# Scoring both heads of an attention pair with 64-row products, the causal mask added to the gate row, and the weight sums of the MLP moved behind the attention

## The chip, the cores and the metric

The kernel runs on one core of one Trainium2 chip. The metric is device time in microseconds (us); before the change the median of three runs is 1742.12 us, with 1740.56 and 1743.21 us at the ends. A core has TensorE (PE: products, and PEld: the loads of their stationary operand), VectorE (DVE), ScalarE (ACT), GpSimd (POOL) and SyncE (SP), whose queue issues every DMA of this kernel.

## The reference

One layer of a hybrid decoder for one sequence of 1024 tokens of width 1024, in float32. A conditioning vector gives shifts, scales and gates. One input projection feeds 16 state-space heads (a chunked scan, "SSD") and 16 attention heads of width 64. The attention is what the change touches; for each block of 128 queries it is

```
logits = einsum('bqhd,bkhd->bhqk', q[:, q0:q1], k[:, :q1]) * d ** -0.5
logits = logits + (cum[:, :, q0:q1, None] - cum[:, :, None, :q1])   # cum: summed log forget gates
logits = where(arange(q0, q1)[:, None] >= arange(q1)[None, :], logits, -inf)
out    = einsum('bhqk,bkhd->bqhd', softmax(logits), v[:, :q1])
```

A term that is the same for all keys of a query drops out of the softmax, so only the key's part of `cum` is needed. The two head groups are normed, joined, and projected by `w_out`; then come a LayerNorm, an MLP of width 4096 with squared ReLU, and a second LayerNorm.

## The kernel before, in words

Each number is kept as a high part (fp32r) and a low part, the remainder, and a product of two numbers is three products of parts: high by high, high by low, low by high. A projection of one 128-column tile over 512 tokens is 8 x 3 products, all 128x128 by 512 columns (`proj`). A planner orders the instructions of each engine from a simulated timeline, by the order in which the program names them and by when operands and buffers come free; the engines then run their lists in that order, and so does SP with its DMAs. `tc.issue_after(x)` (`after` here) keeps DMAs behind `x` in SP's list.

The stages are: conditioning and projections with the SSD scan (to about 385 us), the attention (to about 916 us), the output projection with its norm (to about 1124 us), and the MLP with the second norm. The MLP's products use sums of blocks of its weights (a seven-product scheme): `w2_sums` loads 1 MB of `w2`, makes four differences of 128x512 on POOL, and stores 1 MB to a DRAM scratch `w2t`. There are 14 such calls, two per head pair in the first seven pairs of the attention. They use the buffers `ex` (two).

In the attention, the heads go in 8 pairs. `qkv(p)` projects q, k and v of a pair; it is a generator, advanced in pieces of half a projection (`PIECES`), so that TensorE has these products between those of the attention proper (for the last pair, `out_ssm`, the first half of the output projection). q and k come out with head 0 on partitions 0 to 63 and head 1 on 64 to 127. For each head a tile `q_st` or `k_st` is made that holds the high part in the head's own 64 partitions and the low part in the other 64 (ACT copies the product to `qk_e`, POOL writes the high part, DVE the low part: two 64x512 instructions each per half). One 128-row product of `q_st` with `k_st` is then high by high plus low by low; for the cross terms `swap` makes a copy of the 256 queries with the halves exchanged, by two DMAs of 64 KB, and a second 128-row product uses that copy.

A unit is a head and a group `g` of two query blocks (`tb` = 2g and 2g+1). Pairs run `g` from 0 to 3. `probs` does, for a block of W = 128 (tb + 1) keys, two products per 512 keys, and on the last 128 keys one bf16 product with the identity that adds the mask. Then DVE adds the gate row `cum` and takes the maximum in one pass over W columns (line 519, from PSUM tag `S`, two buffers of 1024 columns: one per head and block), negates the maximum (line 521), ACT takes the exponential and its sum, DVE the reciprocal, and POOL multiplies (line 524). `weigh` transposes the 128x128 blocks on TensorE (line 546), splits them (ACT 548, DVE 549) and multiplies them with v into `o_ps`. The unit after is started before a unit is weighed. `cum` is one row of the DRAM scratch `rowd`, loaded to all partitions, one per head, two buffers.

Of the kernel before, what the change touches and what calls it, by code (L numbers as in the profile page):

```python
# [8 lines left out]
F32 = mybir.dt.float32  # L9
# [3 lines left out]
ALU = mybir.AluOpType  # L13
# [14 lines left out]
NEG = -1.0e30  # L28
# [4 lines left out]
def layer_kernel(ctx, tc, x, xT, cols, rows3, w_ada, b_ada, w_in, w_dtf, w_out, ln_rows, w1, w2, out):  # L33
# [27 lines left out]
    def mm(o, l, r, start, stop):  # L61
        nc.tensor.matmul(o, l, r, start=start, stop=stop)  # L62
# [30 lines left out]
    identb = cst.tile([P, P], BF16, name="identb")  # L93
    nc.vector.tensor_copy(identb, identf)
# [7 lines left out]
    nc.gpsimd.affine_select(maskf, maskf, pattern=[[-1, P]], compare_op=ALU.is_ge, fill=NEG, base=0,  # L102
                            channel_multiplier=1)
    maskb = cst.tile([P, P], BF16, name="maskb")
    nc.vector.tensor_copy(maskb, maskf)
# [67 lines left out]
    def w2_sums():  # L173
# [134 lines left out]
    def row_form(first):  # L308

        rows = T4("misc", "rows")  # L310
        for hb in range(2):
# [3 lines left out]
            nc.vector.tensor_copy(rows[:16, hb * 512:hb * 512 + 512], rp[:16])  # L315
        load(rowd[first:first + 16, :], rows[:16])

    row_form(0)

    def forget_rows():  # L320
# [6 lines left out]
        row_form(16)  # L327
# [112 lines left out]
    for p in range(NPAIR - 1):  # L440
        wn = w_prep(w_in[XI + p + 1])[0]
# [10 lines left out]
    def qkv(p, st):  # L452
# [3 lines left out]
        for n, idx, scale in (("q", KI + p, 0.125), ("k", VI + p, 1.0), ("v", None, None)):  # L456
            w, _ = ws[-1]
            if idx is not None:
                ws.append(w_prep(w_in[idx]))
                marks["w"] = ws[-1][1]  # L460
                st[n] = ts = [R4("qk", f"{n}_st") for _ in range(2)]
# [3 lines left out]
            for half in range(2):  # L465
# [5 lines left out]
                if idx is not None:  # L471
                    e = sm.tile([P, 512], F32, name="qk_e", tag="o_half", bufs=2)
                    nc.scalar.activation(e, o, AF.Copy, scale=scale)
                    for h in range(2):
                        mine = slice(h * 64, h * 64 + 64)
                        other = slice(64 - h * 64, 128 - h * 64)
                        t = ts[h]
# [16 lines left out]
    def probs(st, h, g, cum):  # L494

        q1, k = st["q"][h], st["k"][h]
        q2 = st["q2"].pop((h, g))
        out = []
        for i in range(2):
            tb = 2 * g + i  # L500
            W = (tb + 1) * P
            if g >= 2:
                sp = PT("S", "s_ps", (P, 1024))
                pt = T4("P", "probs")[:, :W]
            elif i == 0:
                sp2 = PT("S", "s_ps", (P, 1024))
                pt2 = T4("P", "probs")
                sp, pt = sp2, pt2[:, :W]
            else:
                sp, pt = sp2[:, 512:], pt2[:, W - P:2 * W - P]  # L510
            for s0 in range(0, W, 512):
                s1 = min(W, s0 + 512)
                last = s1 == W
# [5 lines left out]
            nc.vector.tensor_tensor_reduce(out=pt, in0=sp[:, :W], in1=cum[:, :W], op0=ALU.add,  # L519
                                           op1=ALU.max, scale=1.0, scalar=-3.0e38, accum_out=m[:, 0:1])  # L520
# [726 lines left out]
```

## Time and profile before

| | us |
|---|---|
| median of three runs | 1742.12 |
| the profiled execution | 1744.44 |
| its span, first to last instruction | 1742.7 |
| PE busy | 1654.0 (95%) |
| DVE busy | 1229.9 (71%) |
| POOL busy | 821.6 (47%) |
| ACT busy | 747.2 (43%) |

The profile is of one execution. A product is in flight far longer than it holds the array, so that PE counts as busy while products overlap; how fast products follow each other is read from their start times. A mean in ns is the time of one instruction, not the distance to the next. Idle time is given with what ended it.

### The profile page before, as it was taken

How to read it: one execution, taken by the hardware profiler on the slowest of the kernel's cores; microseconds unless marked ns; L12 is line 12 of the kernel's file. 1: busy time of each engine (PE TensorE's matmuls, PEld its weight loads, DVE VectorE, ACT ScalarE, POOL GpSimd, SP SyncE). 2: the span in 40 equal slices, each digit the busy share in tenths (PEclk: the TensorE clock that was granted, in tenths of full speed). 3: DMA queues.
4: the chain of work that ended last, by engine and by line, in shares of the span. 5: the costliest groups of instructions: out<-in, count | busy, mean ns of one | idle time of the engine just before them, and what ended most of it. 6: DMA issues, size and time to landing. Idle time of an engine off the chain costs nothing.

```text
span 1742.7 us, 22932 instructions
## 1 busy us (share of the span) xinstructions
PE 1654.0 (95%) x8316; PEld 1368.7 (79%) x8316; DVE 1229.9 (71%) x1898; ACT 747.2 (43%) x1321; POOL 821.6 (47%) x670
## 2 busy tenths in 40 slices
PE   8989899899999999999899999799999999999996
PEld 6777787788877878888778887688888878888885
DVE  7755777686777777676665379986767855646668
ACT  3458355414444444444565334633332334343322
POOL 5121332256566466454442345566656624704535
PEclk9999999999999999999999999899999999999998
DMA  8134343334444534434324644043444596676512
GB/s 331 37 123 147 109 145 109 121 130 151 161 142 170 169 134 167 137 121 132 119 97 130 221 157 169 37 175 133 146 143 160 172 340 212 247 242 205 194 36 96
DMA packets 112032, 268.72 MB, mean 154 GB/s; under 512 B 10128, under 2 KB 37008, under 8 KB 111920
## 3 DMA queue, kind: packets, MB, share of 16 engines
q1 hardware_dynamic: 111920, 267.27, 44.2%
q8 instruction: 65, 1.06, 0.3%
q14 instruction: 47, 0.39, 0.1%
HBM read 194.22 MB, written 64.62 MB: 149 GB/s over the span
## 4 chain that ended last, share of the span: by engine, by line
PE 60%; DVE 15%; DMA 8%; ACT 7%; POOL 5%; issue 4%; SPq 0%; DVEq 0%; ACTq 0%; POOLq 0%
PE mm_ps L62 18%; PE f_ps L957 15%; PE s_ps L1073 9%; PE y_ps L1073 7%; PE s_ps L62 5%; PE o_ps L62 4%; DVE ada_red L134 3%; PE t_ps L546 3%; DMA w_b<-in_w_dram 2%; ACT scores L417 2%; POOL w_b L182 2%; DMA raw_ada<-in_w_ada_dram 1%; DVE w_hl L85 1%; DVE conv_a L346 1%; DVE h_hl L85 1%
## 5 line engine op out<-in xcount | busy, mean ns | idle before, releaser
L62 PE MATMUL mm_ps<-h_hl,w_hl 128*128 128x512 f32 x2016 | 504.5, 400 | 10.9 <-POOL w_hl L79 6.1
L62 PEld LDWEIGHTS mm_ps<-h_hl,w_hl 128*128 128x128 f32 x2016 | 373.5, 191 | 88.3 <-POOL w_hl L79 6.9
L85 DVE TENSOR_TENSOR w_op<-raw_w,w_op 128x512 fp32r<-128x512 f32 (+1 forms) x149 | 186.9, 1260 | 23.2 <-ACT w_op L81 22.6
L957 PE MATMUL f_ps<-h_s,w_op 128*128 128x512 f32 x768 | 183.8, 394 | 6.4 <-ACT h_s L81 3.3
L957 PEld LDWEIGHTS f_ps<-h_s,w_op 128*128 128x128 f32 x768 | 146.0, 190 | 38.4 <-ACT h_s L81 3.7
L524 POOL TENSOR_SCALAR probs<-probs,m 128x128 f32<-128x128 f32 (+7 forms) x128 | 104.5, 822 | 127.3 <-DVE m L523 122.8
L81 ACT CAST w_op<-raw_w 128x512 fp32r<-128x512 f32 (+1 forms) x149 | 114.5, 774 | 100.2 <-PE f_ps L957 53.0
L1073 PE MATMUL s_ps<-w_op,a_op 128*128 128x512 f32 x672 | 153.7, 390 | 1.5 <-DVE a_op L85 1.1
L1073 PEld LDWEIGHTS s_ps<-w_op,a_op 128*128 128x128 f32 x672 | 125.9, 188 | 28.8 <-DVE a_op L85 1.6
L79 POOL TENSOR_SCALAR w_hl<-raw_w 128x512 fp32r<-128x512 f32 x86 | 60.5, 705 | 180.0 <-PE mm_ps L62 126.1
L85 DVE TENSOR_TENSOR a_op<-a_ld,a_op 128x1024 fp32r<-128x1024 f32 x53 | 75.5, 1427 | 98.4 <-ACT a_op L81 98.4
L132 POOL TENSOR_TENSOR raw_ada<-raw_ada,c_act 128x1024 f32<-128x1024 f32 x44 | 88.8, 2027 | 117.1 <-DMA raw_ada<-in_w_ada_dram 99.8
L522 ACT ACTIVATE probs<-probs,m 128x128 f32<-128x128 f32 (+7 forms) x128 | 99.1, 775 | 96.8 <-DVE m L521 86.5
L957 PE MATMUL f_ps<-h_hl,w_op 128*128 128x512 f32 x576 | 136.9, 389 | 0.0
L85 DVE TENSOR_TENSOR w_hl<-raw_w,w_hl 128x512 fp32r<-128x512 f32 x88 | 81.5, 929 | 68.5 <-POOL w_hl L79 68.2
L548 ACT CAST pt_hl<-t_ps 128x512 fp32r<-128x512 f32 (+1 forms) x160 | 84.8, 542 | 100.7 <-PE t_ps L546 97.3
L957 PEld LDWEIGHTS f_ps<-h_hl,w_op 128*128 128x128 f32 x576 | 108.0, 188 | 22.4
L81 ACT CAST a_op<-a_ld 128x1024 fp32r<-128x1024 f32 x53 | 55.7, 1054 | 159.7 <-PE s_ps L1073 80.7
L62 PE MATMUL o_ps<-pt_hl,v_s 128*128 128x256 f32 (+1 forms) x640 | 110.9, 300 | 8.7 <-DVE pt_hl L549 5.4
L549 DVE TENSOR_TENSOR pt_hl<-t_ps,pt_hl 128x512 fp32r<-128x512 f32 (+1 forms) x160 | 99.6, 630 | 23.1 <-ACT pt_hl L548 21.6
L519 DVE CUSTOM_DVE_ANT_0 probs<-s_ps,cumrow 128x128 f32<-128x128 f32 (+7 forms) x128 | 94.8, 750 | 28.9 <-PE s_ps L62 20.1
L1073 PE MATMUL y_ps<-w_op,a_op 128*128 128x512 f32 x504 | 114.7, 389 | 0.0
(254 smaller groups left out, 3136.1 us busy)
## 6 DMA issues: line engine op xcount, KB each, us to landing
raw_w<-in_w_dram SPq DMA_DIRECT2D x57, 512.0 KB, 4.3
a_ld<-ad SPq DMA_DIRECT2D x49, 512.0 KB, 4.4
raw_ada<-in_w_ada_dram SPq DMA_DIRECT2D x48, 512.0 KB, 3.6
raw_w<-in_w_in_dram SPq DMA_DIRECT2D x44, 512.0 KB, 3.7
w_b<-in_w_dram SPq DMA_DIRECT2D x14, 1024.0 KB, 8.0
w2t<-w_b SPq DMA_DIRECT2D x14, 1024.0 KB, 4.3
ad<-a_s SPq DMA_DIRECT2D x28, 512.0 KB, 3.4
raw_w<-w2t SPq DMA_DIRECT2D x28, 512.0 KB, 4.8
```

The lines of the kernel that those rows point to most:

```text
L62: nc.tensor.matmul(o, l, r, start=start, stop=stop)
L79: nc.gpsimd.tensor_scalar(hi, raw, 1.0, 1.0, op0=ALU.mult, op1=ALU.mult)
L81: nc.scalar.copy(hi, raw)
L85: eng.tensor_tensor(lo, raw, hi.bitcast(F32), op=ALU.subtract)
L132: nc.gpsimd.tensor_tensor(raw, raw, c_act.unsqueeze(2).broadcast_to([P, KT, P]), op=ALU.mult)
L519: nc.vector.tensor_tensor_reduce(out=pt, in0=sp[:, :W], in1=cum[:, :W], op0=ALU.add, op1=ALU.max, scale=1.0, scalar=-3.0e38, accum_out=m[: ...
L522: nc.scalar.activation(pt, pt, AF.Exp, bias=m[:, 1:2], scale=1.0, accum_out=m[:, 2:3])
L524: nc.gpsimd.tensor_scalar(pt, pt, m[:, 3:4], 1.0, op0=ALU.mult, op1=ALU.mult)
L548: nc.scalar.copy(hl[:, 0, :n], tp[:, :n])
L549: nc.vector.tensor_tensor(hl[:, 1, :n], tp[:, :n], hl[:, 0, :n].bitcast(F32), op=ALU.subtract)
L957: nc.tensor.matmul(o, l, r, start=first and k == 0 and m == 0, stop=last and k == 3 and m == 2, skip_group_check=True)
L1073: nc.tensor.matmul(banks[j], ahl[a_][:, n, js], whl[w_][:, n, :], start=first and d == 0 and n == 0 and m == 0, stop=last and d == ND - 1 ...
```

## The change

- `qkv`: q and k of both heads are split together, 128 partitions at a time, by ACT (high part) and DVE (low part, straight from PSUM). q is scaled by -0.125 in place of 0.125. POOL has no part in it. `swap` and its DMAs are gone.
- `probs` takes one block of both heads. Each head's logits are three products of 64 rows (high by high, high by low, low by high); the two heads alternate, head 0 on rows 0 to 63 of the array, head 1 on rows 64 to 127, into a PSUM buffer each. They are named with raised priority, and the first product of a block is made to wait for the DVE pass of the block before it, for its second head.
- All logits are negated: the row form of the forget sums is written with a minus, DVE takes the minimum, ACT the exponential with scale -1. The step that negated the maximum is gone.
- The mask is no product any more: POOL adds `maskf` (1e30 above the diagonal) to the 128 columns of the block's diagonal in `cum`, 128x128 per head and block. For this the groups run from `g` = 3 down to 0, and the later block of a group first. The columns beyond are not read again.
- The softmax tiles come in turn from the two buffers of `ex` (both heads in one) and from `P`.
- `w2_sums` is called behind the attention: two calls after each remaining block of `out_ssm` and two after each of the first three blocks of the second half of the output projection, one with POOL and one with DVE, loads ordered behind the last store of the attention.
- `PIECES` and the points where a pair's projections must be done are set anew for the new order.

```diff
-    def w2_sums():
+    def w2_sums(eng):
...
-        with after(marks["w"]):
+        with after(marks["last"]):
...
-            nc.gpsimd.tensor_tensor(o, x_, y_, op=ALU.subtract)
+            eng.tensor_tensor(o, x_, y_, op=ALU.subtract)
...
-        for n, idx, scale in (("q", KI + p, 0.125), ("k", VI + p, 1.0), ("v", None, None)):
+        for n, idx, scale in (("q", KI + p, -0.125), ("k", VI + p, None), ("v", None, None)):
...
-                    e = sm.tile([P, 512], F32, name="qk_e", tag="o_half", bufs=2)
-                    nc.scalar.activation(e, o, AF.Copy, scale=scale)
-                    for h in range(2):
...
-                        nc.gpsimd.tensor_scalar(t[mine, hs], e[mine, :], 1.0, 1.0, op0=ALU.mult, op1=ALU.mult)
-                        nc.vector.tensor_tensor(t[other, hs], e[mine, :], t[mine, hs].bitcast(F32), op=ALU.subtract)
+                    split(o, st[n][0][:, hs], st[n][1][:, hs], "act", scale=scale)
...
+    def prob_tiles():
+        steps[0] += 1
+        if steps[0] % 2:
+            t = T4("ex", "probs", shape=(P, 2, 1024))
+            return [t[:, 0, :], t[:, 1, :]]
+        return [T4("P", "probs") for _ in range(2)]
...
-                mm(sp[:, s0:s1], q1[:, tb * P:(tb + 1) * P], k[:, s0:s1], True, False)
-                mm(sp[:, s0:s1], q2[:, i * P:(i + 1) * P], k[:, s0:s1], False, not last)
-                if last:
-                    mm(sp[:, tb * P:W], identb, maskb, False, True)
+                for m, (a, b) in enumerate(((qh, kh), (qh, kl), (ql, kh))):
+                    for h in range(2):
+                        hp = slice(h * 64, h * 64 + 64)
+                        ins = mm(u["sp"][h][:, at + s0:at + s1], a[hp, tb * P:(tb + 1) * P], b[hp, s0:s1], m == 0, m == 2)
+                        if s0 == 0 and m == 0 and h == 0 and "ttr" in marks:
+                            tc.add_manual_dep(ins.ins, marks["ttr"].ins.name, ...
...
+            nc.gpsimd.tensor_tensor(cum[:, tb * P:W], cum[:, tb * P:W], maskf, op=ALU.add)
...
-            nc.vector.tensor_scalar(m[:, 1:2], m[:, 0:1], -1.0, None, op0=ALU.mult)
-            nc.scalar.activation(pt, pt, AF.Exp, bias=m[:, 1:2], scale=1.0, accum_out=m[:, 2:3])
+            nc.scalar.activation(pt, pt, AF.Exp, bias=m[:, 0:1], scale=-1.0, accum_out=m[:, 1:2])
...
-    PIECES = {p: (0, 3, 1, 3) for p in range(NPAIR)}
+    PIECES = {p: {3: (1, 1), 2: (2, 2), 1: (2, 2), 0: (2, 2)} for p in range(NPAIR)}
...
-    units = [(p, g, h) for p in range(NPAIR) for g in range(4) for h in range(2)]
+    units = [dict(p=p, g=g, st=sts[p], pts=[[None, None], [None, None]]) for p in range(NPAIR) for g in (3, 2, 1, 0)]
...
+    for i in (1, 0):
+        start(units[0], i)
+    for n, u in enumerate(units):
...
+        for h in range(2):
+            if nxt is not None:
+                if nxt["p"] != p:
+                    fill_to(nxt["p"], K_DONE)
+                start(nxt, 1 - h)
+            for _ in range(PIECES[p][g][h]):
+                next(fill, None)
+            if g == 3 and p:
+                fill_to(p, 99)
+            weigh(u["st"], h, g, u["pts"][h], ops[:, h, :])
```

## Rows read from the trace of the kernel before

**Rows 1.** The page: busy us of each engine, share of the span, instructions.
```profile
PE 1654.0 (95%) x8316; PEld 1368.7 (79%) x8316; DVE 1229.9 (71%) x1898; ACT 747.2 (43%) x1321; POOL 821.6 (47%) x670
```
**Rows 2.** Busy time of the engines in four stretches; columns in the first line.
```profile
core 0: us, PE busy (x) PEld busy (x) DVE busy (x) ACT busy (x) POOL busy (x), PEclk, DMA share, GB/s
0.00:40.00 40.00, 31.39 (x123) 25.35 (x124) 28.29 (x38) 14.44 (x14) 23.23 (x19) 0.91 0.87 336
385.00:916.00 531.00, 509.03 (x2912) 427.02 (x2911) 384.43 (x889) 255.62 (x548) 287.55 (x307) 0.98 0.42 142
916.00:1080.00 164.00, 160.88 (x769) 133.21 (x768) 103.75 (x137) 72.74 (x134) 68.30 (x53) 1.00 0.53 174
1200.00:1240.00 40.00, 40.00 (x178) 33.10 (x177) 29.19 (x30) 12.59 (x22) 25.55 (x17) 1.00 0.41 145
```
**Rows 3.** The chain of work that ended last, 385 to 916 us, by line.
```profile
by line: PE mm_ps L62 33.8%; PE o_ps L62 11.8%; PE s_ps L62 10.2%; PE t_ps L546 8.1%; DMA w_b<-in_w_dram 5.6%; POOL w_b L182 4.8%; issue 3.1%; DVE probs L519 2.7%; DVE ada_red L134 2.6%; DVE pt_hl L549 2.2%; POOL probs L524 1.8%; DVE w_hl L
```
**Rows 4.** A wait of TensorE, 385 to 916 us: us, times, longest.
```profile
PE s_ps L62 <- DVE m L519: 3.7, 8, 0.7
```
**Rows 5.** TensorE's groups, 385 to 916 us: busy us, mean ns, idle before.
```profile
L62 PE MATMUL mm_ps<-h_hl,w_hl 128*128 128x512 f32 x1062 | 269.6, 399 | 0.0
L62 PE MATMUL o_ps<-pt_hl,v_s 128*128 128x256 f32 x601 | 103.9, 300 | 8.3 <-DVE pt_hl L549 5.1 <-DVE y_attT L566 2.5 <-ACT pt_hl L548 0.4
L546 PE MATMUL t_ps<-identf,probs 128*128 128x128 f32 x546 | 87.3, 279 | 3.3 <-DVE pt_hl L549 2.6 <-DVE v_s L490 0.3 <-POOL probs L524 0.2
L62 PE MATMUL s_ps<-k_st,q_st 128*128 128x512 f32 (+3 forms) x192 | 70.7, 373 | 3.9 <-DVE m L519 3.7
...
L62 PE MATMUL mm_ps<-wo_hl,y_hl 128*128 128x512 f32 x88 | 24.3, 408 | 2.7 <-POOL wo_hl L85 1.0 <-ACT wo_hl L81 0.6 <-DVE wo_hl L88 0.5
```
**Rows 6.** TensorE in order of time around two runs of 64-column products: start, us.
```profile
122.32 1.32 PE L62 MATMUL mm_ps<-h_hl,w_hl 128*128 128x512 f32 x5
123.56 0.43 PE L62 MATMUL s_ps<-scores,xc 128*64 128x128 f32 x2
123.93 2.83 PE L62 MATMUL mm_ps<-h_hl,w_hl 128*128 128x512 f32 x11
...
152.95 1.50 PE L62 MATMUL s_ps<-xd,b_nat 128*128 128x128 f32 x12
154.38 1.97 PE L62 MATMUL s_ps<-scores,xc 128*64 128x128 f32 x32
156.28 0.73 PE L62 MATMUL mm_ps<-h_hl,w_hl 128*128 128x512 f32 x2
```
**Rows 7.** TensorE in order of time: a score product; after its mask, the next.
```profile
604.25 0.40 PE L62 MATMUL s_ps<-k_st,q 128*128 128x512 f32 x1
...
604.61 0.30 PE L546 MATMUL t_ps<-identf,probs 128*128 128x128 f32 x1
```
**Rows 8.** VectorE's groups by shape, 385 to 916 us.
```profile
L549 DVE TENSOR_TENSOR pt_hl<-t_ps,pt_hl 128x512 fp32r<-128x512 f32 x90 | 61.1, 684 | 13.6 <-ACT pt_hl L548 12.8
...
L479 DVE TENSOR_TENSOR q_st<-qk_e,q_st 64x512 fp32r<-64x512 f32 x28 | 26.1, 931 | 1.8 <-POOL q_st L478 1.0
...
L519 DVE CUSTOM_DVE_ANT_0 probs<-s_ps,cumrow 128x1024 f32<-128x1024 f32 x15 | 18.2, 1216 | 3.9 <-PE t_ps L546 3.8
L521 DVE TENSOR_SCALAR m<-m 128x1 f32<-128x1 f32 x127 | 17.8, 146 | 0.9
```
**Rows 9.** GpSimd's groups by shape, 385 to 916 us.
```profile
L182 POOL TENSOR_TENSOR w_b<-w_b 128x512 f32<-128x512 f32 x52 | 71.1, 1375 | 13.8 <-DMA w_b<-in_w_dram 10.7 <-DVE m L523 2.2
...
L478 POOL TENSOR_SCALAR q_st<-qk_e 64x512 fp32r<-64x512 f32 x28 | 20.1, 719 | 7.1 <-ACT qk_e L473 6.0
...
L524 POOL TENSOR_SCALAR probs<-probs,m 128x128 f32<-128x128 f32 x16 | 6.4, 401 | 16.6 <-DVE m L523 16.3 <-PE s_ps L62 0.2
```
**Rows 10.** DMA issues of the page: count, KB each, us to landing.
```profile
w_b<-in_w_dram SPq DMA_DIRECT2D x14, 1024.0 KB, 8.0
...
q<-q_st SPq DMA_DIRECT2D x128, 64.0 KB, 2.6
```

More of the change, by code (lines that the diff above doesn't have):

```diff
@@ L27 @@
 RMS_EPS = 1e-5
-NEG = -1.0e30
+BIG = 1.0e30
 TAPS = None
@@ L61, in mm @@
     def mm(o, l, r, start, stop):
-        nc.tensor.matmul(o, l, r, start=start, stop=stop)
+        return nc.tensor.matmul(o, l, r, start=start, stop=stop)
     def load(o, i):
@@ L306, in layer_kernel, with row_form @@
     rowd = dr.tile([32, T], F32, name="rowd")
-    def row_form(first):
+    def row_form(first, sign):
         rows = T4("misc", "rows")
@@ L460, in qkv @@
                 marks["w"] = ws[-1][1]
-                st[n] = ts = [R4("qk", f"{n}_st") for _ in range(2)]
+                st[n] = [R4("qk", f"{n}_hl") for _ in range(2)]
             else:
@@ L492, in qkv @@
             yield
[L494 to L510, printed above, removed]
+    steps = [0]
@@ new lines, in prob_tiles, with probs @@
+    def prob_tiles():
[4 more added lines that the diff above has]
+        return [T4("P", "probs") for _ in range(2)]
+    def probs(u, i):
+        st, g = u["st"], u["g"]
+        tb = 2 * g + i
+        W = (tb + 1) * P
+        if g >= 2 or "sp" not in u:
+            u["sp"] = [PT("S", "s_ps", (P, 1024)) for _ in range(2)]
+            u["pt"] = prob_tiles()
+        at = 0 if g >= 2 else i * 512
+        (qh, ql), (kh, kl) = st["q"], st["k"]
+        with tc.high_priority(offset=500):
@@ L521, in probs @@
[L521 to L535 removed]
+                for m, (a, b) in enumerate(((qh, kh), (qh, kl), (ql, kh))):
[3 more added lines that the diff above has]
+                        if s0 == 0 and m == 0 and h == 0 and "ttr" in marks:
+                            tc.add_manual_dep(ins.ins, marks["ttr"].ins.name,
+                                              mybir.DependencyInfo(mybir.DependencyClass.Sync, mybir.DependencyReason.DATA),
+                                              reason="both heads' banks are free")
@@ L688, in layer_kernel, with start @@
             ada_some(1)
-    units = [(p, g, h) for p in range(NPAIR) for g in range(4) for h in range(2)]
+    units = [dict(p=p, g=g, st=sts[p], pts=[[None, None], [None, None]]) for p in range(NPAIR) for g in (3, 2, 1, 0)]
     cums = {}
     ys = {}
-    def start(unit):
-        p, g, h = unit
-        if g == 0 and h == 0:
+    def start(u, i):
+        p = u["p"]
+        if p not in cums:
+            cums[p] = []
             for hh in range(2):
@@ L719, in fill_to @@
             next(fill)
-    swap(sts[0], 0, 0)
-    swap(sts[0], 1, 0)
-    pts = start(units[0])
-    ops = None
-    for n, (p, g, h) in enumerate(units):
-        if g == 3 and h == 1 and p + 1 < NPAIR:
-            fill_to(p + 1, QK_DONE if p + 1 < NPAIR - 1 else 99)
-        if n + 2 < len(units):
-            p2, g2, h2_ = units[n + 2]
-            if g2 == 0 and h2_ == 0:
-                fill_to(p2, Q_DONE)
-            swap(sts[p2], h2_, g2)
-        nxt = start(units[n + 1]) if n + 1 < len(units) else None
-        for _ in range(PIECES[p][g]):
-            next(fill, None)
-        if g == 0 and h == 0 and p:
-            fill_to(p, 99)
-        if h == 0:
-            ops = PT("o", "o_ps", (P, 2, 256))
-        weigh(sts[p], h, g, pts, ops[:, h, :])
-        if h == 1:
-            finish(p, g, ops, ys[p])
-            if g in (1, 3) or p == 7:
-                ada_some(2)
-            if g in (0, 2) and p < 7:
-                w2_sums()
-        pts = nxt
+    for i in (1, 0):
+        start(units[0], i)
+    for n, u in enumerate(units):
+        p, g = u["p"], u["g"]
+        nxt = units[n + 1] if n + 1 < len(units) else None
+        ops = PT("o", "o_ps", (P, 2, 256))
+        for h in range(2):
+            if nxt is not None:
[7 more added lines that the diff above has]
+            weigh(u["st"], h, g, u["pts"][h], ops[:, h, :])
+        finish(p, g, ops, ys[p])
+        if g in (0, 2) or p == 7:
+            ada_some(2)
     g2t = cst.tile([P, 8], F32, name="g2t")
@@ L864, in layer_kernel @@
             u = u_pre(tb + 1)
+        if tb < 3:
+            w2_sums(nc.gpsimd)
+            w2_sums(nc.vector)
     adr = [dr.tile([7, P, 2, 512], F32, name=f"ad{i}") for i in range(ND)]
```

53 lines of the change are left out of this document (18 added, 35 removed).

## The prediction, as it went on record before the changed kernel was run

> **What bounds the kernel now.** I read the page first: PE is busy for 95% of the span (its weight loads, which run beside its products, for 79%), the next engine, DVE, for 71% [rows 1]. Then a table by stage, because a share over the whole span mixes stages. In the attention (385 to 916 us) PE is busy 509 of 531 us, DVE 384, POOL 288; in the output projection behind it PE 161 of 164 us, DVE 104, POOL 68 [rows 2]. TensorE sets both. But "busy" is not "at its pace". The pace stands in a stretch where nothing disturbs PE: 178 products of 512 columns in 40.0 us, 0.225 us each, at a granted clock of 1.00 [rows 2]. Narrow full-array products go no faster than 0.11 us: twelve from 152.95 us, the next group at 154.38, which is 0.119 each with the change of group in it [rows 6]. So I take 0.225, 0.169, 0.1125 and 0.11 us for 512, 384, 256 and 128 columns.
>
> At this pace the attention's list would take: 1150 wide products (1062 + 88) x 0.225 = 259 us; 601 of `o_ps` x 0.1125 = 68; 546 transposes x 0.11 = 60 [rows 5]; the scores with their masks 86 (below); the other hundred or so of the 2912, 11. Sum 484 of 531 us. The remaining 47 us are idle (22), restarts after waits, and some time at half clock (granted 0.98 in the mean, so below 2.4 GHz for a few stretches). That is all that relief of the other engines can give.
>
> Where does the relief lie? The chain that ended last, in this stretch, runs over the weight sums: 5.6% on their loads and 4.8% on their POOL instructions, 55 us of 531 [rows 3]. POOL works in order: a softmax multiply behind a `w_b` difference that still waits for its DMA waits too, and the transposes after it. PE covers most of that with projections.
>
> **The change part by part.**
>
> *The score products.* A pair has 12 chunks of keys per pass over its 8 blocks: six of 512 columns, two each of 384, 256 and 128. One product over each is 6 x 0.225 + 2 x (0.169 + 0.1125 + 0.11) = 2.13 us. Before, two heads with two products each: 4 x 2.13 x 8 pairs = 68 us. A mask costs what it delays the next start: 0.36 us from a 512-column product over its mask to the next, less 0.225, is 0.135 us [rows 7]; 128 of them are 17 us (8 us if one costs only the 0.06 of a half-array product, rows 6). Before: 86 us (76 to 86).
>
> After, six products per chunk for two heads, each with half of the rows. The trace has none of 64 rows, but it has 64-column ones of alternating halves: 32 of 128 columns from 154.38 to 156.28 us, 0.059 us each against 0.119 for the full-array ones before them [rows 6]. Two halves take the time of one whole: they run side by side. If row halves do the same, a pair of them costs what one product cost: 3 x 2.13 x 8 = 51 us. Lower bound: this. Upper: no overlap, 102 us. Between: only the loads of stationary operands go one after the other, no pair under 2 x 0.11 us: 36 pairs per head pair at 0.225 x 8 = 65 us. I take 51, the nearest row.
>
> Going into half-array products and out again is not free. Five wide products from 122.32 us should have let the next start at 123.45; it started at 123.56. Two halves (0.12) should have ended at 123.68; the next wide one started at 123.93 [rows 6]. That is 0.36 us for one excursion. The wide one after the long run shows one more part: its successor starts 0.33 us behind it (0.73 less the 0.40 of one, rows 5 and 6), 0.1 over the pace. So 0.25 to 0.47 us; I take 0.36. There is one run per block, 64 of them, if the planner keeps them whole: 23 us (16 to 30). After: 74 us. The step gives -11 us (ends: 51 + 16 - 86 = -19 and 65 + 30 - 76 = +19; without overlap 102 + 23 - 86 = +39).
>
> *A rule against it.* In rows 2 a wide product hides its weight load entirely, same rows of the array or not (PEld 33.1 us busy beside 178 products in 40.0). The Trainium skill ("TensorE: Matmul & The Clock Gate", Part 3, The mechanism) says that a weight load overlaps products in flight only when their row groups differ. By that rule, with both row halves in flight, each pair would also pay a load. It is a rival below.
>
> *q and k split for both heads.* DVE: 64 instructions of 64x512 at 0.93 become 32 of 128x512; nearest row the one that also reads PSUM, 0.684 [rows 8]: -60 + 22 = -38 us. POOL: 64 x 0.72 = -46 us [rows 9]. ACT unchanged. The projection's only bank is now held until DVE has read it, 0.7 us longer, 32 times; the next half projection is behind other products in PE's list, which cover it. Uncovered it would be 22 us.
>
> *Negated logits.* 128 negations go: -18 us of DVE [rows 8].
>
> *Mask on POOL.* 128 additions of 128x128, not in the trace: between a multiply of that size, 0.40, and a four times larger two-operand one, 1.375 [rows 9]; I take 0.6, near the former: +77 us (51 to 176). The DVE pass must wait for it. It can run from the end of the previous pass of its head, beside the block's own products (0.33 us for the smallest run, 1.35 for the largest), so mostly hidden; where POOL is on a 1.4 us instruction, not.
>
> *Swaps.* 128 DMAs of 64 KB leave SP's list [rows 10]; PE hardly waited for them. Nothing.
>
> *The wait for both passes.* A run's first product waits for both DVE passes of the block before, where each head had its own buffer. Behind it in PE's list everything waits. DVE passes take up to 1.2 us [rows 8]; before, PE waited for them 8 times, 3.7 us in all [rows 4]. The planner puts the run where it expects the pass to be over: I take +4 us (0 to 48, rival below).
>
> *Sums moved.* The attention loses 71 us of POOL [rows 9] and 28 DMAs of 1 MB [rows 10]. With the other edits POOL goes from 288 to about 248 us, DVE from 384 to 328. How much of the 47 us does that give back? At least none, at most some 35 (products will still restart after waits). Since a tenth of the chain lay on the sums, a quarter: -10.
>
> Behind the attention, 14 calls: by the generator's count ten fall into blocks 3 to 7 of the first half, four into the second half. 28 differences each for DVE (at 0.684, +19 on 104) and POOL (at 1.375, +39 on 68) fit into 164 us. DMA is tighter: 174 GB/s x 164 us is 28.5 MB, plus 29.4 MB makes 58; at the rate of the first stretch (336 GB/s at a share of 0.87, so 386 at most) that is 150 of 164 us [rows 2]. The `y_raw` and weight loads that feed PE share SP's list and the engines with it. +5 us (0 to +25).
>
> **Sum**: -11 - 10 + 4 + 5 = -12 us from the profiled execution's 1744.4 (span 1742.7 and 1.7 around it), 1732. That execution lies 2.3 us over the median of 1742.1, so 1730.
>
> **The rivals.**
> 1. *Deeper relief.* Nearly all that is not pace comes back: -35 in place of -10, nothing lost behind: 1742 - 11 - 35 + 4 = 1700. For it: the chain over `w_b`. Against: only 22 us of the stage are idle on PE.
> 2. *A wash.* The restarts eat the score gain (30 for 23) and relief is small: 1742.
> 3. *The weight sums jam the output projection*: SP's list blocks behind loads waiting for `ex`, `y_raw` comes late, +25 in place of +5: 1750. For it: a DMA share of 0.9. Against: only two buffers, so the calls throttle themselves.
> 4. *The double wait takes over (slower).* If at each of 64 runs PE finds the second pass, 0.75 us in the mean, still to come and nothing else before it in its list, +48 in place of +4: 1774. It decides from about 0.25 us per run (+16), where the gain is gone. Against: 3.7 us now.
> 5. *Row halves do not run side by side*: +39 for -11: 1780. Against: column halves do.
> 6. *Each pair pays a weight load*: 288 pairs x 0.11 = +32: 1762. Against: plain products hide it, and 32 half-array products in 1.90 us leave no room for it. This is the time by the skill's rule named above; the trace disagrees so far, but it shows no row halves.
>
> **How the numbers follow.** Chances: forecast 0.44 (own range 1714 to 1738), deeper relief 0.14, wash 0.14, jam 0.10, double wait 0.08, no overlap 0.06, weight loads 0.04. Under 0.2% (3.5 us) a time of this kernel can't be told from no change. Faster 0.44 + 0.14 = 0.58, same 0.14, slower 0.28. The range for 8 in 10 reaches from the relief to the jam and the weight loads: 1702 to 1764.
>
> **What would show it.** Right: score products in pairs that start together, a run over 1024 keys under 2 us; 64 runs; PE's stretch of the attention shorter by some 20 us; DVE there near 330, POOL near 250; PE still gapless behind it at a DMA share near 0.9. Wrong: starts within a run 0.2 us apart for every product; more than 64 runs; idle time of PE before score products of over 10 us, ended by DVE or by the mask's POOL addition; idle time before the output projection's products ended by DMA.

## The result: 1809.3 us, slower by 3.9%

The changed kernel takes 1809.3 us in the median of four runs (1807.0 to 1813.4), the kernel before beside it 1741.7: ratio 1.0392, 95% interval 1.0376 to 1.0408. The forecast was 1730, the range ended at 1764. It is wrong in sign.

The page's line of busy times, to be held against [rows 1]:

```profile
PE 1661.3 (92%) x8380; PEld 1356.9 (75%) x8380; DVE 1210.7 (67%) x1764; ACT 743.6 (41%) x1321; POOL 806.2 (45%) x706
```

VectorE and GpSimd have less to do than before, and the kernel is slower all the same: the relief came, and the time did not. By stage, to be held against [rows 2] (attention, output projection, transition to the MLP in three pieces, the MLP's first stage at pace):

```profile
core 0: us, PE busy (x) PEld busy (x) DVE busy (x) ACT busy (x) POOL busy (x), PEclk, DMA share, GB/s
385.00:975.00 590.00, 545.30 (x3158) 440.18 (x3157) 351.57 (x759) 269.33 (x576) 241.15 (x331) 0.97 0.22 74
975.00:1139.00 164.00, 144.19 (x647) 118.35 (x646) 127.70 (x146) 56.23 (x109) 100.12 (x72) 0.95 0.87 305
...
1300.00:1340.00 40.00, 40.00 (x178) 33.15 (x177) 33.75 (x36) 12.77 (x24) 31.54 (x20) 1.00 0.50 177
...
1000.00:1010.00 10.00, 2.93 (x7) 2.35 (x8) 3.05 (x4) 3.20 (x5) 2.71 (x3) 0.61 1.02 357
1040.00:1100.00 60.00, 53.52 (x251) 43.64 (x249) 58.40 (x69) 21.73 (x49) 41.15 (x30) 1.00 0.81 289
...
1152.00:1186.00 34.00, 9.78 (x28) 6.59 (x29) 24.20 (x29) 19.84 (x48) 24.04 (x13) 0.50 0.21 78
```

Where the time went is read from three marks of TensorE: the attention's last product with v, the last product of the output projection, and a fixed product (the 97th) of the MLP's first stage; each mark is a start, in us.

| | attention ends | output projection | transition | rest |
|---|---|---|---|---|
| before | 950.3 | +143.5 | +38.0 | 610.9 |
| changed | 974.5 | +164.5 | +55.6 | 610.5 |

So 24 us are lost in the attention and 39 behind it. The sums may start only behind the last store of the attention. The 164 us in which the prediction placed them [rows 2] begin at 916 us, 34 us ahead of the attention's last product; in the kernel before, only 144 us lie between that product and the last of the output projection:

```profile
950.00:1094.00 144.00, 140.57 (x654) 116.04 (x653) 97.28 (x126) 60.01 (x119) 71.85 (x53) 1.00 0.53 178
```

In the changed kernel the sums' first load is issued at 977 us and their last difference starts at 1155, 16 us into the transition. TensorE waits there as follows (wait, us, times, longest; 975 to 1195 us). 34 us of the transition run at 1.2 GHz (granted 0.50): the clock fell while TensorE stood idle (1150.3 to 1160.9 us), and stood at 0.97 from 1186 to 1195, when products ran on end again.

```profile
PE t_ps L789 <- ACT h_t L796: 16.0, 4, 10.6
PE mm_ps L62 <- ACT y_hl L81: 9.7, 1, 9.7
PE t_ps L789 <- DVE u L753: 8.5, 3, 5.3
PE f_ps L940 <- ACT h_s L81: 8.2, 1, 8.2
```

The wait for `y_hl` is one for a DMA: ScalarE makes `y_hl` from `y_raw`, whose load was issued at 1000.52 us between two loads of the sums (998.70 and 1001.63), with the DMA share at 1.02:

```profile
1006.40 1.66 ACT L81 CAST y_hl<-y_raw 128x512 fp32r<-128x512 f32 x3 [8.09 <-DMA y_raw<-yd]
```

In the attention the same view (385 to 975 us) shows the wait that the prediction looked at, `s_ps` for `m`, hardly grown against [rows 4]; what grew is waiting for the splits of the softmax:

```profile
PE t_ps L535 <- DVE pt_hl L538: 13.3, 11, 3.9
PE o_ps L62 <- DVE pt_hl L538: 6.5, 6, 3.7
PE s_ps L62 <- DVE k_hl L85: 4.9, 3, 2.0
PE s_ps L62 <- DVE m L519: 4.2, 11, 0.7
...
PE mm_ps L62 <- DVE q_hl L88: 2.0, 1, 2.0
```

TensorE's groups there, as in [rows 5]. The score products' busy time, 74.0 us for 576, says little; their start-to-start times sum to 87.3 us in 77 runs, against 89.4 with the masks before (without TensorE's idle time 69 against 87):

```profile
L62 PE MATMUL mm_ps<-h_hl,w_hl 128*128 128x512 f32 x1064 | 271.5, 403 | 2.0 <-DVE q_hl L88 2.0
L62 PE MATMUL o_ps<-pt_hl,v_s 128*128 128x256 f32 (+1 forms) x640 | 113.0, 299 | 9.6 <-DVE pt_hl L538 6.5 <-ACT pt_hl L537 2.6
L535 PE MATMUL t_ps<-identf,probs 128*128 128x128 f32 x576 | 90.7, 283 | 18.3 <-DVE pt_hl L538 13.3 <-DVE v_s L479 3.8 <-POOL raw_ada L128 1.2
L62 PE MATMUL s_ps<-k_hl,q_hl 64*128 64x512 f32 (+3 forms) x576 | 74.0, 368 | 9.2 <-DVE k_hl L85 4.9 <-DVE m L519 4.2
```

One run of twelve 64-row products in the order of time (start, us), to be held against [rows 6, 7]: 1024 keys of both heads in six pairs of 512 columns, 804.48 to 806.06, that is 1.58 us:

```profile
803.95 0.60 PE L535 MATMUL t_ps<-identf,probs 128*128 128x128 f32 x4
804.48 1.65 PE L62 MATMUL s_ps<-k_hl,q_hl 64*128 64x512 f32 x12
806.06 0.73 PE L62 MATMUL mm_ps<-h_hl,w_hl 128*128 128x512 f32 x2
```

The two products of a pair of 512 columns mostly start 2 to 4 ns apart: row halves do run side by side. Inside a run such pairs follow at 0.232 us, but the first takes 0.335 and the last 0.327; and the wide product ahead of a run takes 0.319, the one behind it 0.336, against 0.227 elsewhere (medians of this trace at full clock, waits left out). So a run costs some 0.40 us beyond its pairs, half of it at its neighbours.

VectorE's and GpSimd's new forms came as sized from [rows 8, 9] (0.684 and 0.6 us); the moved loads landed in 8.5 us, 8.0 before [rows 10]:

```profile
L88 DVE SCALAR_TENSOR_TENSOR q_hl<-mm_ps,q_hl 128x512 fp32r<-128x512 f32 x14 | 9.6, 685 | 5.4 <-ACT q_hl L87 5.4
...
L517 POOL TENSOR_TENSOR cumrow<-cumrow,maskf 128x128 f32<-128x128 f32 x126 | 60.7, 487 | 154.6 <-DVE m L519 133.7 <-DMA cumrow<-rowd 19.9
...
w_b<-in_w_dram SPq DMA_DIRECT2D x14, 1024.0 KB, 8.5
```

### The profile page after: what moved, and what is told of

Its sections match the earlier page's. It is cut to its first block, busy times and chain, and to the rows that moved or that the text cites. A ratio compares the mean times of both kernels' runs of the same rounds, so it can differ in the third digit from the quotient of the medians.

```text
span 1805.1 us, 22750 instructions
## 1 busy us (share of the span) xinstructions
PE 1661.3 (92%) x8380; PEld 1356.9 (75%) x8380; DVE 1210.7 (67%) x1764; ACT 743.6 (41%) x1321; POOL 806.2 (45%) x706
## 4 chain that ended last, share of the span: by engine, by line
PE 59%; DVE 16%; DMA 8%; ACT 8%; issue 4%; POOL 3%; SPq 1%; DVEq 0%; ACTq 0%; POOLq 0%
PE mm_ps L62 18%; PE f_ps L940 14%; PE s_ps L1056 8%; PE y_ps L1056 6%; PE s_ps L62 5%; PE o_ps L62 3%; DVE ada_red L130 3%; DMA raw_ada<-in_w_ada_dram 3%; PE t_ps L535 3%; ACT scores L413 2%; POOL raw_ada L128 1%; DMA w_b<-in_w_dram 1%; DVE h_hl L85 1%; DMA y_raw<-yd 1%; DVE w_b L178 1%
## 5 line engine op out<-in xcount | busy, mean ns | idle before, releaser
L517 POOL TENSOR_TENSOR cumrow<-cumrow,maskf 128x128 f32<-128x128 f32 x128 | 62.0, 490 | 162.9 <-DVE m L519 133.7
L519 DVE CUSTOM_DVE_ANT_0 probs<-s_ps,cumrow 128x896 f32<-128x896 f32 (+7 forms) x128 | 92.2, 752 | 59.1 <-PE s_ps L62 41.8
L521 ACT ACTIVATE probs<-probs,m 128x896 f32<-128x896 f32 (+7 forms) x128 | 99.1, 776 | 65.0 <-DVE m L519 64.8
L81 ACT CAST a_op<-a_ld 128x1024 fp32r<-128x1024 f32 x53 | 55.6, 1053 | 159.7 <-PE s_ps L1056 79.3
L523 POOL TENSOR_SCALAR probs<-probs,m 128x896 f32<-128x896 f32 (+7 forms) x128 | 99.9, 788 | 33.3 <-DVE m L522 32.6
```

Of the source, the lines that this page charges most:

```text
L81: nc.scalar.copy(hi, raw)
L517: nc.gpsimd.tensor_tensor(cum[:, tb * P:W], cum[:, tb * P:W], maskf, op=ALU.add)
L519: marks["ttr"] = nc.vector.tensor_tensor_reduce(out=pt, in0=sp, in1=cum[:, :W], op0=ALU.add, op1=ALU.min, scale=1.0, scalar=3.0e38, accum_ ...
L521: nc.scalar.activation(pt, pt, AF.Exp, bias=m[:, 0:1], scale=-1.0, accum_out=m[:, 1:2])
L523: nc.gpsimd.tensor_scalar(pt, pt, m[:, 2:3], 1.0, op0=ALU.mult, op1=ALU.mult)
```

## The experiments

Ratios are to the kernel before, run beside each kernel; "attention", "output", "transition" are the marks above.

### What the weight sums cost behind the attention

**The kernel before with the sums moved alone.**

```
-            if g in (0, 2) and p < 7: w2_sums()
+  (behind out_ssm's blocks and blocks 0 to 2 of the second half)  w2_sums(nc.gpsimd); w2_sums(nc.vector)
```

> The kernel before with one part of the change alone: the 14 weight sums moved behind the attention, at the same places and engines as in the changed kernel. Theory A (the moved sums cost what lies behind the attention: from the last o_ps product to the MLP's 97th f_ps product the changed kernel takes 220 us, the one before 182): about 38 us slower than before, 1780 (1768 to 1790), DMA share near 0.9 and PE waits of 10 us for y_hl and h_t behind the attention. Theory B (the new form of the attention delays what follows it, the sums are hidden): within 5 us of before.

1775.8 us, 1.0190 [1.0170, 1.0211]: theory A. The attention ends at 933.6 with 20 more products of the output projection done (4.5 us at 0.225): 21 us gained. Output +161.7 for 558 products in place of 578, transition +68.0: 53 us lost (18.2 + 4.5 + 30.0). Half of the whole loss is this move. The two stages behind the attention:

```profile
934.00:1095.00 161.00, 143.53 (x626) 116.27 (x625) 125.83 (x146) 53.39 (x105) 97.39 (x71) 0.94 0.84 300
1095.00:1163.00 68.00, 29.84 (x114) 22.81 (x113) 44.71 (x54) 27.80 (x62) 32.58 (x24) 0.67 0.29 107
```

**The changed kernel without the differences** (loads and stores of the sums stay; the four subtractions of each are left out).

> The changed kernel with the four differences of each weight sum left out; the loads and stores of 1 MB stay, so the scratch holds the loaded blocks and the MLP computes with wrong weights. It parts what the moved sums cost into transfers and arithmetic. If the transfers jam the output projection (DMA share 0.87 there): at most 10 us faster, 1799 to 1809. If DVE and POOL do (DVE is 9.9 of 10 us busy from 1040 to 1150): 20 us or more faster, 1775 to 1790.

1785.6, 1.0256 [1.0229, 1.0283]; output +152.1, transition +47.7. The second case holds: about 20 of the 39 us go with the differences on VectorE and GpSimd. The rest stays with the transfers: TensorE's wait for `y_hl` stays (10.6 us for 9.7, at a DMA share of 0.97 from 972 to 1124 us), while the one for `h_t` falls from 16.0 to 6.3.

**The changed kernel with the sums back in the attention**, on GpSimd, at groups 1 and 3, sharing the two buffers of `ex` with the softmax.

> The changed kernel with the sums back in the attention, on POOL, two per head pair (behind groups 1 and 3); they share the two ex buffers with the softmax tiles there. Theory A: the stretch behind the attention falls back from 220 to about 182 us; the attention itself stays some 24 us over before or gets up to 15 us worse by the shared buffers and POOL: 1771 to 1786. Theory B: no better than 1800.

1792.4, 1.0287 [1.0268, 1.0306], between the two theories. The stages behind are as before (+146.7, +37.4), and the attention ends 22 us later (996.3). The stages, with GpSimd's work back in the first line:

```profile
385.00:996.00 611.00, 556.39 (x3161) 449.57 (x3160) 358.77 (x759) 269.58 (x575) 315.43 (x387) 0.96 0.35 119
996.00:1143.00 147.00, 142.04 (x652) 116.67 (x651) 100.87 (x126) 59.67 (x120) 73.09 (x54) 0.99 0.53 179
1143.00:1180.00 37.00, 27.38 (x113) 21.66 (x113) 35.77 (x49) 23.64 (x51) 19.25 (x14) 0.82 0.07 29
```

With the sums in the attention the new form ends it at 996 and the old one at 950; with the sums outside, at 974.5 and (20 products taken off) 929. The new form costs some 45 us there, with the sums inside as with the sums behind.

### What the new form costs in the attention

**Gate sums at another place.** `ada_some(2)`, two column reductions of 1.9 us on VectorE, ran after groups 1 and 3; the change has them after 0 and 2, and group 0 is now the last of a pair. This run puts them after 1 and 2.

> The changed kernel with one edit: the conditioning sums (ada_some) are called behind groups 1 and 2 of a pair in place of groups 0 and 2. Theory A (in the attention the 24 us come from four or five pair borders at which two 2 us DVE reductions stand ahead of the splits of the transposed softmax blocks, PE waiting 3.5 to 3.9 us each time with no projection at hand): the long waits go, 1790 to 1800. Rival C (at the border PE has no other work whatever DVE does, because the next projection's weights come late): the waits stay under another name, 1805 to 1812.

1797.0, 1.0312 [1.0284, 1.0340]; attention 961.9: theory A, 12.6 us come back in the attention. In both kernels the sums had the second and the fourth place in a pair; what is new is that the fourth now stands ahead of group 3, the heaviest, and no longer ahead of group 0. In the changed kernel's VectorE at a pair's border (start, us), the splits stand behind two reductions:

```profile
621.57 3.72 DVE L130 TENSOR_REDUCE ada_red<-raw_ada 128x128 f32<-128x1024 f32 x2
625.22 0.40 DVE L555 TENSOR_TENSOR y_attT<-o_ps,o_half 64x256 f32<-64x256 f32 x1
625.55 0.14 DVE L522 RECIPROCAL m<-m 128x1 f32<-128x1 f32 x1
625.62 1.26 DVE L538 TENSOR_TENSOR pt_hl<-t_ps,pt_hl 128x512 fp32r<-128x512 f32 x2
```

and TensorE, in the same microseconds, waits for the first of these splits:

```profile
621.50 0.96 PE L62 MATMUL s_ps<-k_hl,q_hl 64*128 64x512 f32 x6 [0.39 <-DVE m L519]
626.33 1.50 PE L535 MATMUL t_ps<-identf,probs 128*128 128x128 f32 x7 [3.87 <-DVE pt_hl L538]
```

**The same with other pieces**: `PIECES` 3: (3, 2), 2: (2, 2), 1: (1, 1), 0: (2, 2).

> The changed kernel with ada_some behind groups 1 and 2 (797 us less than 2600: 1797 alone) and more projection pieces in the heaviest group: PIECES 3:(3,2), 2:(2,2), 1:(1,1), 0:(2,2) in place of 3:(1,1), 2:(2,2), 1:(2,2), 0:(2,2). Theory D (the new attention is slow because the softmax-times-v products of group 3, 3.4 us per head, have too few projections beside them): the last o_ps product at 945 to 955 us in place of 962, total 1780 to 1790. Rival E (the slowness is in the score runs and what they break up): within 4 us of 1797.

(In its text, 1797 is the time of the run above.) 1790.3, 1.0275 [1.0246, 1.0304]; the attention ends where it did (961.6), so the distribution of the projections is not the cause there. The 7 us of the total lie in the transition (55.1 in place of 61.2), which neither theory had, and the two intervals overlap.

**Without the added wait** (`add_manual_dep` out; gate sums as in the last two).

> The changed kernel with ada_some behind groups 1 and 2, and without the added wait of a block's first product for both passes (each product then waits for its own head's bank alone; the priority stays). Theory E1 (the double wait stalls PE): 5 to 15 us under 1797. Theory E2 (the wait keeps runs whole and costs little): as many or more runs of 64-row products than 77, and 1797 to 1810.

1809.4, 1.0391 [1.0364, 1.0418]: 12 us slower than with it, theory E2. The planner then starts one head's products before the other's bank is free; runs go from 78 to 103 and their start-to-start sum from 72.9 to 106.1 us. Taking the wait away gains nothing; it holds the runs together.

**Order and mask as before** (groups 0 to 3, mask as a bf16 product, old pieces and gate sums; heads paired, 64 rows).

> The changed kernel with the groups in the old order, 0 to 3, the old pieces and the old places of ada_some, and the mask again a bf16 product per head; the 64-row products of both heads, the q and k split, the negated logits, the softmax tiles and the place of the sums stay as changed. If the new order (with the mask that needs it) makes the attention slow: the last o_ps product falls from 974 to about 930 to 940 us, the value of the kernel before with the sums moved, and the total to 1765 to 1775. If the 64-row scoring itself does: 960 or later, total over 1795.

1825.2, 1.0485 [1.0458, 1.0512]; attention 992.2. The reversed order and the mask on GpSimd, taken together, are not the loss: without them it grows by 16 us, near the 17 that the prediction set down for the mask's products. The two were not taken apart.

**128-row products in the place of the 64-row ones**, on the kernel with the gate sums moved. Two products per head and chunk over all 128 rows.

```
-  enumerate(((qh, kh), (qh, kl), (ql, kh)))       a[hp, ...], b[hp, s0:s1]
+  enumerate(((qh, kh), (qh, kl)))                 a[:, ...],  b[:, s0:s1]
```

> The changed kernel with the gate sums moved (1797), its score products taken over all 128 rows, two for each head and 512 keys (384 in all) in place of three 64-row products for each head (576): the scores then mix both heads and lack a term, everything around them (both heads together, both S banks, the split, the order) stays. Theory A (entering and leaving the 64-row form delays the products around some 78 runs by 0.2 to 0.4 us each): the products' own starts sum to about 82 in place of 73, the other products of the attention fall by 15 to 30 us, and the attention ends 5 to 20 us earlier; total 1777 to 1792. Rival B (the row form costs nothing outside its runs; the loss is waiting, for both banks and for what VectorE has queued): the attention ends 8 to 12 us later; total 1805 to 1810.

1790.0, 1.0274 [1.0249, 1.0300]; attention 958.1, 4 us earlier: the direction of theory A, short of its size. The products' own starts sum to 85.3 us in place of 72.9, and all others of the stage to 488 in place of 502: what the 64-row form saves in its runs, 12 us (6 of them idle time), comes back around them, 14 us over 78 runs, 0.18 each, near the 0.20 that the two neighbours of a run pay above. The interval overlaps with that of the 64-row kernel: the form brings nothing that can be measured.

**The heads apart.** The same products, but each head's two blocks are scored by themselves, a bank each, and the next scores of a head are due when that head is weighed; the added wait of a block's first product goes with it.

```
-   u["sp"] = [PT("S", ...) for _ in range(2)]     # a block, both heads; start(nxt, 1 - h)
+   bank = PT("S", ...)                            # a head, block by block; start(nxt, h)
```

> The kernel with 128-row products in the changed kernel's place (1790, attention end at 958 us; the same part of the scores is left out and mixed), and each head's two blocks scored by themselves: a product needs one S bank, not both, and head 0 is weighed while only its own next scores are due. Theory A (the rest of the new form's loss is that both heads' banks must be free together): the attention ends at 940 to 950, total 1772 to 1782, where the old form with the sums behind it took 1776. Rival B (pairing costs nothing; it is the split from the mm bank, the mask on GpSimd or the order of groups): end 952 to 962, total 1784 to 1795.

1769.3, 1.0161 [1.0143, 1.0179]; attention 940.6: 20 us back, theory A. TensorE's wait for the DVE pass, first with the heads together, then apart:

```profile
PE s_ps L62 <- DVE m L519: 11.5, 15, 1.7
```

```profile
PE s_ps L62 <- DVE m L515: 1.5, 4, 0.5
```

With two `S` buffers, two heads scored together take both: nothing can be scored while VectorE reads either. A head at a time, one is filled while the other is read. That is 10 of the 17.5 us in the attention. Some 5 more are the clock: the trace has TensorE at 1.2 GHz for 20.5 us of the attention with the heads together and for 10.2 apart.

This kernel still ends the attention 11.5 us later than the kernel before with the sums moved (940.6 against 929), though it has no mask products. TensorE waits longer for the splits of the softmax; first the kernel before with the sums moved (385 to 934 us), then this one (385 to 941):

```profile
PE t_ps L546 <- DVE pt_hl L549: 1.2, 2, 1.0
```

```profile
PE t_ps L531 <- DVE pt_hl L534: 12.6, 10, 3.9
```

Its total is the lower one only because the transition takes 52.3 us in place of 68.0; why, no run shows. (Order and mask as before has 68.1 there as well.)

**Negated logits alone**, on the kernel before.

> The kernel before with the negated logits alone: 128 negations on VectorE of 146 ns (17.9 us of busy time) go, everything else stays. Theory A (the chain from the row's minimum to the weights is waited for, VectorE has the least room in the attention): 3 to 8 us less, 1734 to 1739. Rival B (PE never waited for these; 5.2 us of a pair's VectorE work in 70 is hidden): 1740 to 1744, no difference.

1738.3, 0.9982 [0.9970, 0.9994]: theory A at its lower end, some 3 us, with an interval just clear of 1. Of the parts run by themselves on the kernel before it is the only one that is not slower.

### Is there a place for the sums?

**In the MLP's first stage, in halves on GpSimd**, on the kernel before.

> The kernel before with the weight sums taken out of the attention and made in the first stage of the MLP, one per pair of weight tiles, in two halves of 256 columns, all on POOL. The kernel before with the sums moved ended its attention 17 us earlier with 20 more products of the output projection done (about 21 us), and paid 53 us behind it. Theory: the attention's 21 us come back and the MLP's first stage, where PE is gapless, DMA at 0.41 and POOL at 0.62, hides most of the sums: 1720 to 1732. Rival (POOL or the shared buffers become the bound there): 1740 to 1770.

1754.0, 1.0073 [1.0049, 1.0097], in the rival's range: the MLP pays 29 us.

**Ahead of the attention**, two calls a round in its seven rounds: the kernel before, then the changed kernel with the gate sums moved.

> The kernel before with the fourteen weight sums moved ahead of the attention: two calls at the end of each of the seven rounds that prepare the state-space part (40 to 385 us of the span), where GpSimd was busy 11 to 20 us in each 60 and the DMA share was 0.17 to 0.48. Theory A (the sums cost the attention about 21 us on GpSimd and only their place behind the attention was costly): the attention ends about 21 us earlier, the output projection and the transition last as before (143 and 38 us), the stage ahead pays at most 8; total 1720 to 1730, 0.988 to 0.993 of before. Rival B (any stage pays for the sums, as the MLP's did with 29 us, since GpSimd makes the high halves of each pair's weights here): the stage ahead is 20 to 29 us longer; total 1740 to 1752.

> The changed kernel with the gate sums moved to groups 1 and 2 of a pair (that kernel alone took 1797) and the weight sums moved ahead of the attention, as in the other kernel of this set. Theory A (the loss behind the attention is the sums, the loss in it is the new form of the attention): the attention lasts as in that kernel, the output projection and the transition come back to 143 to 150 and 36 to 40 us; total 1756 to 1768, 1.008 to 1.015 of before, and 30 to 40 us above the other kernel of this set. Rival B (the new form itself delays what lies behind the attention): the two stages stay at 165 and 61; total 1790 to 1800.

1752.4, 1.0057 [1.0035, 1.0079], and 1773.7, 1.0178 [1.0151, 1.0205]. In both the stages behind the attention are whole again, here the changed kernel's (theory A on that loss):

```profile
978.00:1124.00 146.00, 140.19 (x647) 115.24 (x647) 101.91 (x126) 59.44 (x119) 72.29 (x53) 1.00 0.53 180
1124.00:1161.00 37.00, 27.48 (x114) 21.83 (x113) 35.78 (x49) 23.75 (x51) 19.16 (x14) 0.82 0.07 29
```

But the stage ahead pays: the first scores start at 408 and 416 us, not at 389 and 387; both totals are above what theory A named, the first just above rival B's range as well. The two kernels stand 21 us apart, not 30 to 40. By the marks the changed kernel's attention ends 17.5 us later (20 products put back), and it starts 8 us later. So the new form's price in the attention, with the gate sums moved, is 33 us with the sums behind (961.9 against 929) and about 9 here. About half of that difference is the clock: from the first score to the last product with v, TensorE is at 1.2 GHz for 27.3 us in the changed kernel with the gate sums moved and for 3.4 us here (6.8 in both of the old form). What keeps the clock up here is not shown.

**Half and half**: one call a round ahead, one a pair; then the same with negated logits.

> The kernel before with its fourteen weight sums shared: one in each of the seven rounds ahead of the attention, one in each of the first seven pairs instead of two. Theory A (a stage hides a first sum and pays for the second): the stage ahead grows by 3 to 6 us in place of 19 to 24, the attention gains 10 of the 21 that leaving out all gave, total 1730 to 1738. Rival B (every sum costs the same 1.3 to 1.5 us wherever it stands): 1742 to 1750.

> Both edits together: the sums shared between the stage ahead and the attention, and the negated logits. By theory A of both: 1722 to 1734, faster than both kernels. By rival B of both: 1742 to 1750. If the edits add, its gain is the sum of the two within 2 us; if both only give VectorE and GpSimd the same room, it is the larger of the two.

1756.2, 1.0090 [1.0070, 1.0110], and 1756.5, 1.0087 [1.0064, 1.0110]. Half the sums delay the scores as much (414 us) as all of them, so the delay does not go by the piece. Both times are above what theory A and rival B named, and the negated logits bring nothing here.

**Stores a round, or a call, later**, with negated logits: half ahead with load, differences and store a round apart; all in the attention, each store issued ahead of the next load; both.

> The kernel before with negated logits, seven of the sums ahead of the attention and seven in it (the form that took 1756), but ahead of it each sum's load, its differences and its store are issued a round apart: the load at a round's end with no order forced on it, the differences behind the next round's weight load, the store at that round's end. Theory A (the 24 us that the stage ahead lost in that form came from SP's queue, where a store that waits for GpSimd stands ahead of the next round's weight loads, not from the sums): the attention starts at 389 to 396 us in place of 416, total 1722 to 1735. Rival B (GpSimd's own time delays the high halves of the weights): it starts at 405 to 418, total 1745 to 1757.

> The kernel before with negated logits (1738), all fourteen sums in the attention as there, but the store of a sum is issued ahead of the next sum's load in place of right behind its own differences; SP's queue waited for these differences 38.0 us in ten waits in the attention of the kernel before. Theory A (these waits delay the weight and row loads behind them and so PE): 1728 to 1735. Rival B (SP's queue is far enough ahead in the attention; what the sums cost there is GpSimd): 1736 to 1741.

> Both edits: seven sums ahead, issued a round apart, and the seven in the attention with the later store. By theory A of both 1718 to 1730; by rival B of the first 1745 to 1757; otherwise within 2 us of the first kernel of this set.

1754.0, 1.0075 [1.0059, 1.0090]; 1739.4, 0.9988 [0.9978, 0.9998]; 1753.3, 1.0071 [1.0054, 1.0089]. The scores start at 403: between the theories. The edit did not do its work: the planner drew the loads forward, and SP's queue ahead of the attention (wait, us, times, longest) waits for the differences longer than in the half-and-half form (24.1) and as long as with all fourteen there (43.2):

```profile
SPq L65 <- POOL w_b L190: 41.2, 7, 10.4
```

Why the stage ahead pays stays open. In the attention the later store does nothing (1738.3 without it).

## Why the prediction was wrong

The loss in steps. The total of a step comes from the ratios at a median of 1742 us and carries some 5 us of uncertainty; the last two columns are its share in the attention and behind it, from the marks of the profiled executions (the 20 products of the output projection put back behind the attention). A profiled execution lies up to 3 us from its kernel's median, so that the columns do not add up exactly.

| step | kernel | ratio | us | attention | behind |
|---|---|---|---|---|---|
| sums behind the attention | before, sums moved | 1.0190 | +33 | -21 | +53 |
| split, mask, negation, order, buffers, pieces | heads apart, 128 rows | 1.0161 | -5 | +12 | -17 |
| both heads at once | 128 rows | 1.0274 | +20 | +18 | +4 |
| 64-row products | gate sums moved | 1.0312 | +7 | +4 | +5 |
| place of the gate sums | changed | 1.0392 | +14 | +13 | -6 |

- **The weight sums: the step that failed first.** "+5 us (0 to +25)" measured +53, -10 measured -21. The terms were sized right: a DMA share of 0.87 for 0.9, VectorE and GpSimd busy 128 and 100 us for 123 and 107. What failed is the argument that they "fit into 164 us". Only 144 us lie behind the attention before, and in these the prediction's own sum for the DMAs (178 GB/s x 144 us and 29.4 MB, at 386 GB/s) is 143 us. A mean over a stage hid 60 us in which VectorE is busy for 58.4, and 10 us at a DMA share of 1.02 in which TensorE waits for `y_hl`. And the sum stopped at the output projection: 18 to 30 us are lost behind it, in the transition, where part of the work then runs at half clock. Rival 3 had half of the mechanism (`y_raw` late), not the size; the other half is the differences on VectorE and GpSimd.
- **The double wait: the second.** The prediction priced the wait in front of a run (+4); that wait stayed at 4.2 us in the changed kernel, and removing it does harm. The price is what it stands for: one buffer pair in place of two buffers, 20 us, shown on the 128-row form and together with the added wait. Rival 4 had named 0.25 us per run as the point where the gain is gone (+16); the measured +20 lies there. It was given 0.08.
- **Split, mask, negation and order: the third.** Their new instructions came as sized (0.685 us for 0.684, 0.487 for 0.6), and the sum gave them gains alone, 17 us of them for the mask's products. In the attention the bundle costs 12 us; that its total is -5 is due to the shorter transition, which was not forecast, so it is luck. Negated logits alone, and order and mask together, are not the loss; split, softmax tiles and pieces were not run by themselves, so this part of the cause stays open.
- **The score products.** Right in form and near in size. Row halves run side by side (rival 5 falls): by the pace of each width the pairs take 53 us, 51 predicted. A run costs 0.40 us for 0.36, and there are 78 for 64 (gate sums moved): 31 us for 23. With the 87 us before (86 predicted) the step is -3 in place of -11. Nearly all of that gain was the mask's: between the products alone, without masks, the prediction's own terms give 51 + 23 - 68 = +6, and 64 rows in place of 128 measured +7. Its floor of 0.11 us for narrow products is none (59 of 127 `o_ps` products of 128 columns before are followed within 0.075 us), worth 3 us at most.
- **Rival 6.** The rule from the Trainium skill ("TensorE: Matmul & The Clock Gate", Part 3, The mechanism), that a weight load overlaps products in flight only when their row groups differ, would have made each pair pay a load. Inside a run pairs follow at 0.232 us, against 0.227 for a wide product elsewhere: the trace does not agree, no load is paid, and rival 6 falls.
- **The place of the gate sums** is not in the prediction at all, though the diff has the line. The calls were read as a count, not as a time at which VectorE is taken for 3.7 us.
- **The clock in the attention** has no term either. From the first score to the last product with v TensorE was at 1.2 GHz for 17 us before and for 31 us in the changed kernel, which is some 7 of the 24 us lost there.

## What to carry to other kernels

Before moving work to a stage with room in the mean, look at that stage in windows of 10 us and at the stage behind it: what is late at the end of a full stretch is paid there. Two results computed at once out of two buffers are single-buffered, whatever the wait in front of them shows. And when a loop's order is turned, re-time everything hung on its index: work that keeps its place can come to stand ahead of the heaviest step.

## What the runs showed of the hardware

- Two 64-row products of 512 columns on different row halves mostly start 2 to 4 ns apart, and such pairs follow at 0.232 us in a run; but a run costs 0.40 us beyond its pairs, 0.20 of it at the products ahead and behind.
- TensorE was granted 1.2 GHz for 34 us on end (1152 to 1186) when the transition left it busy for 9.8 of them; before, the clock there was 0.82 in the mean of 38 us.
